# A written-out order of matrix work for all eight head pairs of a decoder layer

## The chip, the core and the metric

The kernel runs on one core of a Trainium2 chip. A core has a matrix engine (TensorE, PE in the profile; its weight loads are PEld), VectorE (DVE), ScalarE (ACT), GpSimd (POOL) and SyncE (SP), which here only issues DMAs. Each engine works through its own instructions in the order in which they stand, and waits on semaphores for the others. The metric is the device time of one execution in microseconds (us); the kernel before took 1234.75 us, the median of three runs (1234.38 to 1235.01).

## The reference, cut to what matters

One decoder layer over 1024 tokens of width 1024: a norm, one projection to the queries, keys and values of two groups of heads, both groups causal in blocks of 128 queries, an output projection, then a mixture of experts and a gated embedding.

```python
log_keep = jnp.where(strict, jax.nn.log_sigmoid(-z), 0.0)             # group 1: stick-breaking, 8 heads of 64
log_survive = lax.cumsum(log_keep, axis=3, reverse=True) - log_keep
weights = jnp.where(strict, jnp.exp(log_beta + log_survive), 0.0)
...
z = z - slopes[None, :, None, None, None] * dist                      # group 2: differential, 4 heads
probs = jax.nn.softmax(jnp.where(s_pos <= t_pos, z, -jnp.inf), axis=-1)
attn = probs[:, :, 0] - lam * probs[:, :, 1]
...
x = x + jnp.concatenate([_rmsnorm(o_sb), _rmsnorm(o_df)], axis=-1) @ w_out
```

`lam` comes from four vectors of 64 numbers. The results of each group are normed over their features before `w_out`, so sums of squares of the attention results are needed.

## The kernel before

**Pairs and units.** The attention is cut into eight pairs of 128 features. Pairs 0 to 3 hold two stick-breaking heads each, pairs 4 to 7 one differential head each (two score maps). A pair is cut into units of two query blocks (pr = 0 to 3, and by head in pairs 0 to 3). A unit has five kinds of TensorE work:

- score chunks (L361, L362, `z<-K,Qh`): each fills one of three PSUM banks. In pairs 0 to 3 ScalarE reads it twice (L404, L405), VectorE then scans the row (L408) and GpSimd multiplies (L409). In pairs 4 to 7 VectorE adds the distances and takes the maximum (L432), ScalarE takes the exponential (L439), and VectorE joins the two maps (L450).
- turns (L378, `tp<-ident,row`): the finished rows are transposed; ScalarE writes the upper part of the result (`wth`, L54), VectorE the rest (`wtl`, L55).
- values (L488 to L491, `pv<-wth,V` and `pv<-wtl,V`), which need both parts; ScalarE and VectorE evict their sum.
- the finish (L795, `z<-ones,sq`): a sum of squares of the result, after its store to `oT_d` in DRAM.
- beside these, the projections (L228 to L230, `mm<-hT,whi`): the values of this pair and the keys and queries of the next one. One item is six matmuls; four items fill a bank. Each weight matrix is split by ScalarE and VectorE (`wlo`, L201).

**The order.** For pairs 0 to 6 the class `Mix` writes out TensorE's order. It keeps an estimate of the time at which TensorE, ScalarE, VectorE and GpSimd come free, with fixed durations, and takes the next ready item from five queues; a projection is taken when its pair has a smaller share of projections done than of attention, or when nothing else is ready. `allowed` in `run_pairs` holds a unit's scores back until the second last unit is turned; for the first unit of pair 4 until the last unit of pair 3 is turned and pair 3 is finished. Every split and eviction stands behind all that the estimate has given its engine before. The order of the other engines is set by a scheduler with priorities; splits and evictions are raised by `k.boost`.

**Pair 7** is not in this list: when pairs 0 to 6 are done, `attend_items` and `run_items` emit its work beside the output projection's weights (`out_weights`, `woh` and `wol`) and leave TensorE's order to the scheduler. `out.normed(b)` reads `oT_d` back for 128 tokens, takes twelve small VectorE steps from the sums of squares to their inverse roots (L66 to L100), spreads these with transposes (L1130, L1136; L1134 and L1140 after the change), scales the rows (L1132, L1137) and splits them; the output projection (L1158 to L1160) follows.

**Shared places.** `k.sums` (sums of squares of pairs 0 to 3) and `k.dist` (the distances, a GpSimd iota and two VectorE instructions, L807 and L808) have one buffer in turn: `distances` runs when pair 4 begins and has to wait until pair 3's sums are read. `lambdas` runs there too, in a buffer of the ring of rows.

Of the kernel before, what the change touches and what calls it, by code (L numbers as in the profile page):

```python
# [133 lines left out]
def lambdas(k):  # L134
    nc, pool = k.nc, k.cp
    row = k.rows.tile([128, S], FT, name="row")
    lq = row[0:1, 0:256].rearrange("p (a n) -> p a n", a=4)
    for i, a in enumerate((k.lambda_q1, k.lambda_k1, k.lambda_q2, k.lambda_k2)):
        nc.sync.dma_start(lq[:, i, :], a)
    lp = row[0:1, 256:384].rearrange("p (a n) -> p a n", a=2)  # L140
    ls = row[0:1, 384:386]
    for i in range(2):
        nc.vector.tensor_tensor(lp[:, i, :], lq[:, 2 * i, :], lq[:, 2 * i + 1, :], OP.mult)
    nc.vector.reduce_sum(ls, lp, axis=AX)
    nc.scalar.activation(ls, ls, AF.Exp)
# [389 lines left out]
class Mix:  # L535
# [11 lines left out]
    def on(self, eng, ready, dur):  # L547
        self.at[eng] = max(self.at[eng], ready) + dur
        return self.at[eng]

# [25 lines left out]
    def do_s(self):  # L576
        u, c, f, n, last, x = self.S.pop(0)
        f()
        self.pe += c + 0.03
# [4 lines left out]
        if u.P.df:  # L584
            a = self.on("dve", self.pe, dve(w))
            if last:
                d = self.on("dve", a, 0.3)
                e = self.on("act", d, act(n))
                d = self.on("dve", e, 0.2)
# [34 lines left out]
    def do_v(self):  # L624
        u, g = self.V.pop(0)
        u.value(g)
        u.vals += 1
        self.nV += 1
        c = 0.7 if u.P.df else 0.47
        self.pe += c  # L630
        self.done["m", u.p] += c
        if g == u.pr:
            a = self.on("act", self.pe, 0.4)
            self.pvfree = [a if u.P.df else self.on("dve", a, 0.45)]
            u.out = self.pvfree[0]
# [5 lines left out]
    def do_f(self):  # L641
        u = self.F.pop(0)
        u.finish()
        self.on("act", self.pe, 0.4)
# [8 lines left out]
    def do_p(self):  # L653
# [6 lines left out]
        if kind == "last":  # L660
            a = self.on("act", self.pe, 1.2)
            self.mmfree = self.mmfree[1:] + [self.on("dve", a, 1.3)]

# [3 lines left out]

    def run(self):
# [3 lines left out]
        while left():  # L672
            ready = {x: get[x]() for x in left()}
# [13 lines left out]

def run_pairs(k, Ps, qk, n):

    mix = Mix(k, 3)  # L690
    us = [units_of(k, P) for P in Ps[:n]]
    every = [u for x in us for u in x]
# [9 lines left out]

    for p in range(n):
        P, Q = Ps[p], Ps[p + 1]
        v0, v1 = value_projection(k, P)
# [28 lines left out]
        for x in range(2):  # L734
            kd, c, f, ok = turns[x]
            turns[x] = (kd, c, lambda f=f, p=p, x=x: (f(), state["v"].__setitem__((p, x), True)), ok)
        K = group_items(k, lambda Q=Q: Q.W[0], HALVES, evac_k(k, Q))
        QQ = group_items(k, lambda Q=Q: Q.W[1], HALVES, evac_q(k, Q, Q.qscale))
# [10 lines left out]
    for x, u in enumerate(every):  # L749
        near = 1 if u.p == 4 and (u.pr, u.h) == (0, 0) else 2  # L750
        before = every[x - near] if x >= near else None

        def allowed(u=u, before=before, near=near):
            if state["kq"] < u.p or not (before is None or before.turns == before.pr + 1):
                return False
            return near == 2 or not (mix.F and mix.F[0].p < u.p)

        u.allowed = allowed
    return mix
# [18 lines left out]
def finish_o(k, ot, P, pr):  # L778
    nc = k.nc
    q = slice(pr * 256, (pr + 1) * 256)  # L780
    nc.sync.dma_start(k.oT_d[P.ch][:, q], ot)
    if P.df or P.ch:
        sq = k.wk.tile([128, 256], FT, name="sq", bufs=2)
    else:
        sq = k.sums[:, q]
    nc.scalar.activation(sq, ot, AF.Square)
    if not P.df:
        if P.ch:
            nc.gpsimd.tensor_tensor(k.sums[:, q], k.sums[:, q], sq, OP.add)
        if P.ch < 3:  # L790
            return
        sq = k.sums[:, q]
    ps = bank_z(k, P.df)
# [152 lines left out]
def phase_attention(k, moe, pq):  # L946
# [34 lines left out]
    k.nz = 0  # L981
    k.sums = c1.tile([128, S], FT, name="sums")
    k.ss = c1.tile([128, NB, 5], FT, name="ss")
# [3 lines left out]
    def first(p):  # L987
        if p == 1:
            anchor.extend((k.last_hi, k.last_lo) + ((k.last_raw,) if hasattr(k, "last_raw") else ()))
        if p == 4:  # L990
            distances(k)
            lambdas(k)

    mix = run_pairs(k, Ps, qk, 7)
    for u in (mix.S[0][0], *(x[0] for x in mix.S)):
# [16 lines left out]
    v0, v1 = value_projection(k, P)  # L1012
    wo = out_weights(k)
    with ExitStack() as es:
        for x in anchor:
            es.enter_context(tc.issue_after(x.ins))
        out.constants()
    run_items(items[:ends["v"]], v0, wo[:4])
    out.space(0)
    run_items(items[ends["v"]:ends[0]], v1, wo[4:])  # L1020
    out.space(1)
    mid = ends[0] + 2
    run_items(items[ends[0]:mid])
# [976 lines left out]
```

## Time and profile before

| | us |
|---|---|
| median of 3 runs | 1234.75 |
| the profiled execution's own time | 1239.4 |
| its span on the core | 1237.6 |
| TensorE busy in the span | 1154.6 (93%) |
| VectorE busy | 923.6 (75%) |
| ScalarE busy | 721.7 (58%) |
| GpSimd busy | 207.6 (17%) |

The attention of pairs 0 to 3 takes the span from about 40 to 328 us, that of pairs 4 to 7 from 328 to about 597; the output projection runs from 543, the experts from about 715, and the last part from about 1130. A matmul counts as busy until its modelled end, so a busy TensorE can still be slow: the granted clock (PEclk, 1.00 is 2.4 GHz, 0.50 is 1.2 GHz) has to be read beside it.

### The profile page before, as it was taken

How to read it: one execution, taken by the hardware profiler on the slowest of the kernel's cores; microseconds unless marked ns; L12 is line 12 of the kernel's file. 1: busy time of each engine (PE TensorE's matmuls, PEld its weight loads, DVE VectorE, ACT ScalarE, POOL GpSimd, SP SyncE). 2: the span in 40 equal slices, each digit the busy share in tenths (PEclk: the TensorE clock that was granted, in tenths of full speed). 3: DMA queues.
4: the chain of work that ended last, by engine and by line, in shares of the span. 5: the costliest groups of instructions: out<-in, count | busy, mean ns of one | idle time of the engine just before them, and what ended most of it. 6: DMA issues, size and time to landing. Idle time of an engine off the chain costs nothing. (4 is left out here: it accounts for less than half of the span.)

```text
span 1237.6 us, 22827 instructions
## 1 busy us (share of the span) xinstructions
PE 1154.6 (93%) x8181; PEld 831.4 (67%) x8181; DVE 923.6 (75%) x2144; ACT 721.7 (58%) x1408; POOL 207.6 (17%) x298
## 2 busy tenths in 40 slices
PE   5999999999898999989789899999999999997996
PEld 4766666666556666655445488898998989883443
DVE  7577787868466676878797776787878878865875
ACT  6476767666456666743332355676767767653432
POOL 0033433434100000001321111121111211110000
PEclk9999999999998999989899989999999999998999
DMA  6212121211120122523674879899999999947721
GB/s 206 66 30 73 30 73 31 63 36 48 51 75 25 47 61 58 170 71 110 222 216 139 285 229 290 264 341 291 284 324 289 325 292 316 313 135 290 246 77 51
DMA packets 211756, 202.54 MB, mean 164 GB/s; under 512 B 12697, under 2 KB 182681, under 8 KB 211642
## 3 DMA queue, kind: packets, MB, share of 16 engines
q1 hardware_dynamic: 205688, 180.22, 47.1%
q0 software_dynamic: 5808, 20.58, 4.4%
q8 instruction: 65, 1.06, 0.3%
q14 instruction: 49, 0.40, 0.1%
q10 hardware_dynamic: 146, 0.27, 0.1%
HBM read 163.03 MB, written 29.62 MB: 156 GB/s over the span
## 5 line engine op out<-in xcount | busy, mean ns | idle before, releaser
L228 PE MATMUL mm<-hT,whi 128*128 128x512 f32 (+1 forms) x416 | 216.7, 522 | 2.5 <-DVE rs_v L66 1.4
L229 PE MATMUL mm<-hT,whi 128*128 128x512 bf16 (+1 forms) x416 | 157.8, 379 | 4.3 <-DVE hT L184 4.3
L230 PE MATMUL mm<-hT,wlo 128*128 128x512 bf16 (+1 forms) x416 | 156.6, 377 | 0.0
L1607 PE MATMUL gu<-xh,mhiu 128*128 128x128 f32 (+4 forms) x512 | 155.7, 315 | 0.0
L1607 PE MATMUL gu<-xh,mhig 128*128 128x128 f32 (+4 forms) x512 | 154.6, 309 | 0.1
L1609 PE MATMUL gu<-xbl,mhig 128*128 128x128 bf16 (+4 forms) x512 | 125.2, 244 | 2.6 <-DVE xbl L1520 2.6
L1609 PE MATMUL gu<-xbl,mhiu 128*128 128x128 bf16 (+4 forms) x512 | 124.7, 244 | 0.0
L1610 PE MATMUL gu<-xh,mblg 128*128 128x128 bf16 (+4 forms) x512 | 120.1, 235 | 0.0
L1610 PE MATMUL gu<-xh,mblu 128*128 128x128 bf16 (+4 forms) x512 | 119.5, 233 | 0.0
L55 DVE TENSOR_TENSOR mdl<-mrawd,mdh 128x1024 bf16<-128x1024 f32 x63 | 77.0, 1221 | 44.6 <-ACT mdh L54 44.6
L228 PEld LDWEIGHTS mm<-hT,whi 128*128 128x128 f32 x416 | 80.8, 194 | 33.9 <-ACT hT L183 1.9
L54 ACT ACTIVATE wth<-tp 128x512 fp32r<-128x512 f32 (+2 forms) x168 | 71.0, 449 | 55.8 <-PE tp L378 36.2
L55 DVE TENSOR_TENSOR wtl<-tp,wth 128x512 fp32r<-128x512 f32 (+2 forms) x168 | 79.2, 492 | 32.2 <-ACT wth L54 30.9
L409 POOL TENSOR_TENSOR row<-row,keep 128x127 f32<-128x127 f32 (+3 forms) x64 | 77.0, 1204 | 147.0 <-DVE keep L408 90.8
L229 PEld LDWEIGHTS <-whi 128*128 128x128 bf16 x416 | 40.8, 98 | 88.2 <-issue 83.4
L1607 PEld LDWEIGHTS gu<-xh,mhig 128*128 128x128 f32 x512 | 98.1, 192 | 0.9 <-ACT xh L1519 0.5
L55 DVE TENSOR_TENSOR mblg<-mrawg,mhig 128x1024 bf16<-128x1024 f32 x62 | 75.8, 1223 | 30.3 <-ACT mhig L54 29.2
L54 ACT ACTIVATE mdh<-mrawd 128x1024 fp32r<-128x1024 f32 x64 | 67.5, 1055 | 51.7 <-PE ya L1639 47.1
L408 DVE TENSOR_TENSOR_SCAN keep<-keep,zx 128x128 f32<-128x128 f32 (+3 forms) x64 | 85.7, 1346 | 15.5 <-ACT keep L404 15.0
L1607 PEld LDWEIGHTS gu<-xh,mhiu 128*128 128x128 f32 x512 | 97.1, 190 | 0.0
L46 POOL DMA_INDIRECT y_d<-yo,put x27 | 44.5, 1649 | 290.0 <-ACT yo L1657 185.8
L54 ACT ACTIVATE mhig<-mrawg 128x1024 fp32r<-128x1024 f32 x64 | 67.4, 1053 | 20.5 <-PE gu L1610 11.8
(348 smaller groups left out, 3358.7 us busy)
## 6 DMA issues: line engine op xcount, KB each, us to landing
mrawg<-in_w_expert_gate_dram SPq DMA_DIRECT2D x64, 512.0 KB, 5.9
mrawu<-in_w_expert_up_dram SPq DMA_DIRECT2D x64, 512.0 KB, 6.7
mrawd<-in_w_expert_down_dram SPq DMA_DIRECT2D x64, 512.0 KB, 3.7
wraw<-in_w_in_dram SPq DMA_DIRECT2D x24, 512.0 KB, 4.1
yg<-y_d SPq DMA_DIRECT2D x16, 512.0 KB, 5.9
xt<-in_x_dram SPq DMA_DIRECT2D x8, 512.0 KB
oT_d<-ot SPq DMA_DIRECT2D x32, 128.0 KB, 2.9
wraw<-in_w_out_dram SPq DMA_DIRECT2D x8, 512.0 KB, 3.8
```

The lines of the kernel that those rows point to most:

```text
L46: i = k.nc.gpsimd.indirect_dma_start(out=out, out_offset=bass.IndirectOffsetOnAxis(ap=idx, axis=0), in_=src, in_offset=None)
L54: nc.scalar.activation(hi, src, AF.Copy)
L55: (eng or nc.vector).tensor_tensor(lo, src, hi.bitcast(FT), OP.subtract)
L228: nc.tensor.matmul(ps, hi[:, c, :], hT[:, c % 4, :], start=(c == 0), stop=False)
L229: nc.tensor.matmul(ps, wv[:, c, :], k.hT[half][2][:, c, o:o + n], start=False, stop=False)
L230: nc.tensor.matmul(ps, lo[:, c, :], hv[:, c % 4, :], start=False, stop=(c == NC - 1))
L408: nc.vector.tensor_tensor_scan(a, a, k.zeros.to_broadcast([128, n]), 1.0, op0=OP.mult, op1=OP.add)
L409: nc.gpsimd.tensor_tensor(beta[:, :n - 1], beta[:, :n - 1], keep[:, 1:n], OP.mult)
L1607: nc.tensor.matmul(ps[:, x], hi[:, c], xh[:, c], start=(c == 0), stop=False)
L1609: nc.tensor.matmul(ps[:, x], hv[:, c], xl[:, c], start=False, stop=False)
L1610: nc.tensor.matmul(ps[:, x], bl[:, c], xv[:, c], start=False, stop=(c == NC - 1))
```

## The change

Three edits. The sums of squares go to two buffers of their own and the lambdas to a third (these are later taken by the first output weights), and the distances keep a buffer of their own and are made before the first pair. The special rule for pair 4 goes. `Mix` gets a new rule in `on`: a split or eviction marked `first` ends at most 0.7 us later than it would on a free engine, while it still adds its duration to its engine; three small durations of VectorE in the estimate get shorter. And pair 7 joins `Mix`, with its value projection and the output weights in the queue of projections; its items after the finish of its first unit are recorded (`emit`) and emitted beside the output projection.

```diff
 def lambdas(k):
-    row = k.rows.tile([128, S], FT, name="row")
+    row = k.base.tile([128, 512], FT, name="lam", tag="wol2")
...
+    def on(self, eng, ready, dur, first=False):
+        start = max(self.at[eng], ready)
+        self.at[eng] = start + dur
+        return (min(start, ready + 0.7) if first else start) + dur
...
-        u.turn(g)
+        self.emit(0.44, lambda: u.turn(g))
...
-        a = self.on("act", self.pe, 0.6)
-        d = self.on("dve", a, 0.75)
+        a = self.on("act", self.pe, 0.6, True)
+        d = self.on("dve", a, 0.7, True)
...
-            self.pvfree = [a if u.P.df else self.on("dve", a, 0.45)]
+            self.pvfree = [a if u.P.df else self.on("dve", a, 0.45, True)]
...
-    us = [units_of(k, P) for P in Ps[:n]]
+    us = [units_of(k, P) for P in Ps[:n + 1]]
...
+        if p == n:
+            items = group(v0[:4], None, nothing) + [turns[0]] + [("mid", 0.0, f, None) for f in last[0]]
+            items += group(v1[:4], None, nothing) + [turns[1]] + [("mid", 0.0, f, None) for f in last[1]]
...
-        near = 1 if u.p == 4 and (u.pr, u.h) == (0, 0) else 2
-        before = every[x - near] if x >= near else None
...
+        before = every[x - 2] if x >= 2 else None
+        u.allowed = lambda u=u, before=before: state["kq"] >= u.p and (before is None or before.turns == before.pr + 1)
...
-    k.dist = k.ac.tile([128, S], FT, name="sums")
+    k.dist = k.ac.tile([128, S], FT, name="dist")
...
-    k.sums = c1.tile([128, S], FT, name="sums")
+    k.sums = [k.base.tile([128, 512], FT, name=f"sums{x}", tag=f"wol{x}") for x in range(2)]
...
+    distances(k)
+    mix = run_pairs(k, Ps, qk, 7, last)
...
-        mix.run()
-    P = Ps[7]
-    items, ends = attend_items(k, P)
...
+        mix.run(lambda: not mix.P and len(mix.F) <= 3)
+    rest = []
+    mix.emit = lambda c, f: rest.append((c, f))
+    mix.run(lambda: len(mix.F) <= 2)
+    mid = len(rest)
+    mix.run()
     out.normed(0)
-    run_items(items[mid:ends[1]], out.items(0)[1:])
-    run_items(items[ends[1]:], out.items(1) + out.items(2))
+    run_items(rest[:mid], out.items(0)[1:])
+    run_items(rest[mid:], out.items(1) + out.items(2))
```

Place A is on TensorE, in pair 1, at the second head's unit of query blocks 4 and 5: its first turns (`tp`) and its first values (`pv`); the `mm` rows between are projections, ten rows to an item. Before:

```order
L378 MATMUL tp<-ident,row 128x128 x8
L361 MATMUL z<-K_789,Qh_791 128x512
L362 MATMUL z<-K_789,Ql_793 128x512
L364 LDWEIGHTS identb
L364 MATMUL z<-maskb,identb 128x128
L361 MATMUL z<-K_789,Qh_791 128x512
L362 MATMUL z<-K_789,Ql_793 128x512
...
L488 MATMUL pv<-wth,V_796 128x256
L489 MATMUL pv<-wtl,V_796 128x256
```

After the change:

```order
L361 MATMUL z<-K_804,Qh_806 128x512
L362 MATMUL z<-K_804,Ql_808 128x512
L364 LDWEIGHTS identb
L364 MATMUL z<-maskb,identb 128x128
L378 MATMUL tp<-ident,row 128x128 x8
L361 MATMUL z<-K_804,Qh_806 128x512
L362 MATMUL z<-K_804,Ql_808 128x512
...
L488 MATMUL pv<-wth,V_811 128x256
L489 MATMUL pv<-wtl,V_811 128x256
```

Between turns and values stood two score chunks and four projection items (forty rows), and now one chunk and two items (twenty rows).

Place B is on TensorE where pair 3 ends and pair 4 begins; the 256-column chunks without a mask are pair 4's first, L795 is pair 3's last finish. Before:

```order
L795 MATMUL z<-ones,sums 128x1 x2
L361 MATMUL z<-K_3063,Qh_3065 128x256
L362 MATMUL z<-K_3063,Ql_3067 128x256
L361 MATMUL z<-K_3064,Qh_3066 128x256
L362 MATMUL z<-K_3064,Ql_3068 128x256
L361 MATMUL zx<-K_3063,Qh_3065 128x256
L362 MATMUL zx<-K_3063,Ql_3067 128x256
```

After the change:

```order
L488 MATMUL pv<-wth,V_2358 128x256
L489 MATMUL pv<-wtl,V_2358 128x256
L361 MATMUL z<-K_3110,Qh_3112 128x256
L362 MATMUL z<-K_3110,Ql_3114 128x256
L361 MATMUL z<-K_3111,Qh_3113 128x256
L362 MATMUL z<-K_3111,Ql_3115 128x256
L361 MATMUL zx<-K_3110,Qh_3112 128x256
L362 MATMUL zx<-K_3110,Ql_3114 128x256
L488 MATMUL pv<-wth,V_2358 128x256
L489 MATMUL pv<-wtl,V_2358 128x256
```

Pair 4's first scores stood behind all of pair 3, and now stand between values of pair 3's last units but one, with that pair's last unit (its turns and values) still to come.

Place C is on TensorE, from a finish of pair 7 to the first transposes of the output stage (`rs_y`). Before:

```order
L795 MATMUL z<-ones,sq 128x1 x2
L361 MATMUL zx<-K_5159,Qh_5161 128x384
L362 MATMUL zx<-K_5159,Ql_5163 128x384
L361 MATMUL z<-K_5159,Qh_5161 128x512
L362 MATMUL z<-K_5159,Ql_5163 128x512
...
L361 MATMUL z<-K_5159,Qh_5161 128x512
L362 MATMUL z<-K_5159,Ql_5163 128x512
L1130 MATMUL tp<-ident,rs_y 128x128
```

After the change:

```order
L800 MATMUL zx<-ones,sq 128x1 x2
L361 MATMUL z<-K_5148,Qh_5150 128x384
L362 MATMUL z<-K_5148,Ql_5152 128x384
...
L361 MATMUL zx<-K_5148,Qh_5150 128x384
L362 MATMUL zx<-K_5148,Ql_5152 128x384
L1134 MATMUL tp<-ident,rs_y 128x128
L1140 MATMUL tp<-ident,rs_y 128x128 x4
L378 MATMUL tp<-ident,row 128x128 x4
```

Before, this was the finish of pair 7's second unit, and all its scores were done at the first transpose. Now it is the finish of its first unit, with four score chunks between, and the second unit's turns and values and seven score chunks follow behind the transpose.

## Rows read from the trace of the kernel before

**Rows 1.** The page's second part: granted clock, in 40 slices of the span.

```profile
PEclk9999999999998999989899989999999999998999
```

**Rows 2.** Stretches: length; PE, PEld, DVE, ACT, POOL busy (instructions); granted clock; DMA share; GB/s.

```profile
40.00:320.00 280.00, 271.30 (x1615) 179.70 (x1614) 204.92 (x294) 185.60 (x438) 97.19 (x137) 1.00 0.20 52
320.00:360.00 40.00, 35.33 (x171) 20.77 (x170) 23.60 (x76) 21.05 (x49) 2.99 (x9) 0.91 0.16 43
380.00:400.00 20.00, 15.21 (x88) 13.49 (x87) 15.45 (x59) 13.75 (x33) 0.80 (x4) 0.83 0.11 34
500.00:544.00 44.00, 36.95 (x175) 26.18 (x173) 36.64 (x137) 29.90 (x65) 1.41 (x8) 0.84 0.43 139
544.00:600.00 56.00, 53.31 (x296) 32.11 (x294) 43.66 (x167) 20.80 (x42) 6.62 (x11) 0.97 0.38 123
600.00:720.00 120.00, 101.61 (x541) 56.79 (x540) 97.94 (x384) 39.06 (x80) 27.69 (x28) 0.93 0.66 219
```

**Rows 3.** TensorE's waits from 40 to 320 us: total, times, longest.

```profile
PE z L361 <- ACT row L405: 3.4, 3, 1.2
PE pv L489 <- DVE wtl L55: 2.3, 5, 0.8
```

**Rows 4.** TensorE in order of time at pair 4's first scores; idle and releaser in brackets.

```profile
332.51 0.58 PE L361 MATMUL z<-K,Qh 128*128 128x256 f32 x1 [2.70 <-DVE dfm L432]
...
341.70 0.44 PE L378 MATMUL tp<-ident,row 128*128 128x128 f32 x2 [1.62 <-DVE dfm L438]
```

**Rows 5.** VectorE in order of time at the same place: the distances, the first reduction.

```profile
329.98 0.69 DVE L807 TENSOR_SCALAR row<-sums 128x1024 f32<-128x1024 f32 x1 [1.43 <-POOL sums L804]
...
332.15 0.29 DVE L432 CUSTOM_DVE_ANT_0 row<-z,sums 128x128 f32<-128x128 f32 x1 [0.15 <-DVE sums L808]
```

**Rows 6.** TensorE in order of time where pair 4's last unit is turned.

```profile
387.49 0.30 PE L378 MATMUL tp<-ident,row 128*128 128x128 f32 x1 [0.93 <-DVE dfm L437]
391.49 0.90 PE L378 MATMUL tp<-ident,row 128*128 128x128 f32 x3 [3.71 <-DVE row L450]
```

**Rows 7.** TensorE in order of time at place A in pair 1.

```profile
159.28 1.04 PE L378 MATMUL tp<-ident,row 128*128 128x128 f32 x8
...
160.66 0.48 PE L361 MATMUL z<-K,Qh 128*128 128x512 f32 x1
...
161.21 0.39 PE L228 MATMUL mm<-hT,whi 128*128 128x512 f32 x1
...
166.55 0.48 PE L488 MATMUL pv<-wth,V 128*128 128x256 f32 x1
```

**Rows 8.** VectorE in order of time at the same place.

```profile
162.14 1.93 DVE L201 TENSOR_TENSOR wlo<-wraw,whi 128x1024 bf16<-128x1024 f32 x1
...
164.83 1.29 DVE L55 TENSOR_TENSOR wtl<-tp,wth 128x512 fp32r<-128x512 f32 x2
```

**Rows 9.** The weight split L201: count, shortest/median/longest ns, first and last start.

```profile
L201 DVE TENSOR_TENSOR wlo<-wraw,whi x24: 1208/1226/2159, 11.8 to 475.1; 128x1024 bf16<-128x1024 f32 x24
```

**Rows 10.** TensorE in order of time from pair 7's first finish to the output projection.

```profile
523.75 1.01 PE L795 MATMUL z<-ones,sq 128*128 128x1 f32 x4 [0.62 <-ACT sq L786]
...
539.92 0.32 PE L1130 MATMUL tp<-ident,rs_y 128*128 128x128 f32 x1 [0.79 <-DVE rs_y L100]
...
543.44 0.50 PE L1158 MATMUL mm<-woh,od 128*128 128x512 f32 x1 [0.44 <-ACT od L54]
```

**Rows 11.** VectorE in order of time ahead of that transpose.

```profile
529.97 1.22 DVE L1058 TENSOR_TENSOR wol<-wraw,woh 128x1024 bf16<-128x1024 f32 x1
...
531.43 0.55 DVE L432 CUSTOM_DVE_ANT_0 keep<-z,sums 128x384 f32<-128x384 f32 x1
...
531.97 0.17 DVE L66 TENSOR_SCALAR rs_v<-ss 128x10 f32<-128x10 f32 x1
...
539.70 0.17 DVE L100 SCALAR_TENSOR_TENSOR rs_y<-rs_i,rs_y 128x10 f32<-128x10 f32 x1
```

**Rows 12.** ScalarE in order of time in the first stage: first key eviction.

```profile
24.01 0.36 ACT L251 ACTIVATE K<-mm 64x256 fp32r<-64x256 f32 x1
```

More of the change, by code (lines that the diff above doesn't have):

```diff
@@ L545, in __init__ @@
         self.nT = self.nV = 0
-    def on(self, eng, ready, dur):
-        self.at[eng] = max(self.at[eng], ready) + dur
-        return self.at[eng]
+        self.emit = lambda c, f: f()
+    def on(self, eng, ready, dur, first=False):
+        start = max(self.at[eng], ready)
+        self.at[eng] = start + dur
+        return (min(start, ready + 0.7) if first else start) + dur
     def add_pair(self, P, p, units, proj):
@@ L577, in do_s @@
         u, c, f, n, last, x = self.S.pop(0)
-        f()
+        self.emit(c, f)
         self.pe += c + 0.03
@@ L586, in do_s @@
             if last:
-                d = self.on("dve", a, 0.3)
+                d = self.on("dve", a, 0.2)
                 e = self.on("act", d, act(n))
-                d = self.on("dve", e, 0.2)
+                d = self.on("dve", e, 0.15)
                 if x < len(chunks_of(n)):
@@ L625, in do_v @@
         u, g = self.V.pop(0)
-        u.value(g)
+        c = 0.7 if u.P.df else 0.47
+        self.emit(c, lambda: u.value(g))
         u.vals += 1
         self.nV += 1
-        c = 0.7 if u.P.df else 0.47
         self.pe += c
@@ L632, in do_v @@
         if g == u.pr:
-            a = self.on("act", self.pe, 0.4)
-            self.pvfree = [a if u.P.df else self.on("dve", a, 0.45)]
+            a = self.on("act", self.pe, 0.4, True)
+            self.pvfree = [a if u.P.df else self.on("dve", a, 0.45, True)]
             u.out = self.pvfree[0]
@@ L642, in do_f @@
         u = self.F.pop(0)
-        u.finish()
+        self.emit(0.11, u.finish)
         self.on("act", self.pe, 0.4)
@@ L660, in do_p @@
         if kind == "last":
-            a = self.on("act", self.pe, 1.2)
-            self.mmfree = self.mmfree[1:] + [self.on("dve", a, 1.3)]
+            a = self.on("act", self.pe, 1.2, True)
+            self.mmfree = self.mmfree[1:] + [self.on("dve", a, 1.3, True)]
     def share(self, what, p):
@@ L666, in share, with run @@
         return p + (self.done[what, p] / t if t else 1.0)
-    def run(self):
+    def run(self, until=lambda: False):
         do = {"v": self.do_v, "t": self.do_t, "s": self.do_s, "f": self.do_f, "p": self.do_p}
@@ L671, in run @@
         left = lambda: {x: q for x, q in zip("vtsfp", (self.V, self.T, self.S, self.F, self.P)) if q}
-        while left():
+        while left() and not until():
             ready = {x: get[x]() for x in left()}
@@ L685, in run, with run_pairs @@
             do[pick]()
-def run_pairs(k, Ps, qk, n):
+def run_pairs(k, Ps, qk, n, last):
     mix = Mix(k, 3)
-    us = [units_of(k, P) for P in Ps[:n]]
+    us = [units_of(k, P) for P in Ps[:n + 1]]
     every = [u for x in us for u in x]
@@ L701, in proj @@
         return out
-    for p in range(n):
-        P, Q = Ps[p], Ps[p + 1]
+    for p in range(n + 1):
+        P, Q = Ps[p], Ps[min(p + 1, n)]
         v0, v1 = value_projection(k, P)
@@ L736, in run_pairs @@
             turns[x] = (kd, c, lambda f=f, p=p, x=x: (f(), state["v"].__setitem__((p, x), True)), ok)
+        for u in us[p]:
+            u.values = lambda g, p=p: (p, g // 2) in state["v"]
+        if p == n:
+            items = group(v0[:4], None, nothing) + [turns[0]] + [("mid", 0.0, f, None) for f in last[0]]
+            items += group(v1[:4], None, nothing) + [turns[1]] + [("mid", 0.0, f, None) for f in last[1]]
+            mix.add_pair(P, p, us[p], items)
+            break
         K = group_items(k, lambda Q=Q: Q.W[0], HALVES, evac_k(k, Q))
@@ L749, in run_pairs @@
     for x, u in enumerate(every):
-        near = 1 if u.p == 4 and (u.pr, u.h) == (0, 0) else 2
-        before = every[x - near] if x >= near else None
[L753 to L758, printed above, removed]
+        before = every[x - 2] if x >= 2 else None
+        u.allowed = lambda u=u, before=before: state["kq"] >= u.p and (before is None or before.turns == before.pr + 1)
     return mix
@@ L781, in finish_o @@
     nc.sync.dma_start(k.oT_d[P.ch][:, q], ot)
+    sums = k.sums[pr // 2][:, pr % 2 * 256:pr % 2 * 256 + 256]
     if P.df or P.ch:
@@ L784, in finish_o @@
     else:
-        sq = k.sums[:, q]
+        sq = sums
     nc.scalar.activation(sq, ot, AF.Square)
@@ L788, in finish_o @@
         if P.ch:
-            nc.gpsimd.tensor_tensor(k.sums[:, q], k.sums[:, q], sq, OP.add)
+            nc.gpsimd.tensor_tensor(sums, sums, sq, OP.add)
         if P.ch < 3:
             return
-        sq = k.sums[:, q]
+        sq = sums
     ps = bank_z(k, P.df)
@@ L990, in first, with out_constants @@
         if p == 4:
-            distances(k)
             lambdas(k)
-    mix = run_pairs(k, Ps, qk, 7)
+    def out_constants():
+        with ExitStack() as es:
+            for x in anchor:
+                es.enter_context(tc.issue_after(x.ins))
+            out.constants()
+    wo = [f for _, f in out_weights(k)]
+    last = [[out_constants] + wo[:4] + [lambda: out.space(0)], wo[4:] + [lambda: out.space(1)]]
+    distances(k)
+    mix = run_pairs(k, Ps, qk, 7, last)
     for u in (mix.S[0][0], *(x[0] for x in mix.S)):
@@ L1008, in phase_attention @@
     with tc.manual_schedule(engines={mybir.EngineType.PE}):
-        mix.run()
-    P = Ps[7]
-    items, ends = attend_items(k, P)
[L1012 to L1023, printed above, removed]
+        mix.run(lambda: not mix.P and len(mix.F) <= 3)
[4 more added lines that the diff above has]
+    mix.run()
     out.normed(0)
-    run_items(items[mid:ends[1]], out.items(0)[1:])
-    run_items(items[ends[1]:], out.items(1) + out.items(2))
+    run_items(rest[:mid], out.items(0)[1:])
+    run_items(rest[mid:], out.items(1) + out.items(2))
     k.right.close()
```

## The prediction

> **What bounds the kernel now.** I read the page's totals first: TensorE is busy for 1154.6 of 1237.6 us of span, VectorE for 923.6. Then the slices of the granted clock [rows 1]: nearly all nines, with an eight where TensorE had stood still. So the kernel is bound by TensorE, and what can be won is its idle time and the half speed that follows. Third, the stretches [rows 2]: from 40 to 320 us (pairs 0 to 3) TensorE is busy for 271.30 of 280 us at clock 1.00, which leaves 8.7 us over eight units of each pair. The places with a loss are three: 320 to 360 (pair 3 to 4), 380 to 400 (pair 4 to 5), and 500 to 544 (pair 7 and the start of the output stage). Last, I read the engines in order of time at these places.
>
> The profiled execution took 1239.4 us, 4.65 more than the median of 1234.75. The sum is made against its stretches and is then taken off the median.
>
> **Pair 3 to 4: -7.0 us.** Pair 4's first scores wait 2.70 us for a reduction [rows 4], the reduction waits for the distances, and these wait for the iota, which GpSimd could only write when the old sums had been read [rows 5]. A second wait, 1.62 us, follows [rows 4]. In the 40 us, 40 - 35.33 = 4.67 are idle, and 0.09 of the clock is 3.6: 8.3 lost [rows 2]. With a place of its own the distances are there long before, and the order puts pair 4's scores between pair 3's last values (place B), where two other units still have work. Late next is the ordinary chain of a softmax, which has something beside it now; I leave 1.3 for it. Bounds: 8.3 gained, or nothing if values of pair 3 wait there instead.
>
> **Pair 4 to 5: -7.0.** TensorE waits 0.93 and 3.71 us for the last rows of pair 4 [rows 6]; its projections are used up by then, and only turns and values are left. 4.8 idle and 0.17 of 20 us, 3.4, are lost: 8.2 [rows 2]. In the new order two groups of projection items stand between the unit's last scores and its last turns: four items took 166.55 - 161.21 = 5.34 us in pair 1 [rows 7], more than the longest wait. I leave 1.2. Bounds: 8.2, or nothing.
>
> **Pair 7 and the output stage: -3.0.** In 44 us, 7.05 idle and 0.16 of the clock, 7.0: 14.1 lost [rows 2]. Ahead of place C the written order should recover most. But at place C only four score chunks are left between the finish of pair 7's first unit and the first normed transpose, against all of the second unit's rest before, when 16.2 us lay between [rows 10]. From the finish's result VectorE took 7.90 us over the twelve small steps (531.97 to 539.87), with other work between them [rows 11]. Of that work now four reductions of 0.55 (2.2) and one split of 1.22 stand there, with twelve steps of 0.17 (2.0): 5.4 at the least, 7.9 as before; I take 6.6, about the middle, since joined rows come in between too. Four chunks give TensorE 4 x 0.55 (160.66 to 161.21, one chunk) [rows 7] = 2.2: a wait of about 4.5 us in place of 0.79 [rows 10]. The second transposes wait for the scaled rows, as the output projection did for 0.44 [rows 10]; VectorE now has the second unit's rows and lower parts queued there (1.29 a pair [rows 8], twice: 2.6). With 1.2 of small waits and 2.7 of clock, 11 us of loss remain. Bounds: -7 if the moved turns and scores slide in as soon as they are ready, +3 if both waits cost the clock too. The moved items themselves only change places on TensorE.
>
> **Values nearer to their turns: +6.0.** The new estimate lets a lower part end 0.7 us after it is ready at the latest, though VectorE works in its own order. At place A, in pairs 1 to 3: before, the turns start at 159.28 and the values at 166.55, and nothing waits, though VectorE starts the weight split (1.93 us) at 162.14 and the two lower parts at 164.83 only, the first ready at about 164.83 + 1.29/2 = 165.5 [rows 7, 8]. After, one chunk (0.55) comes ahead of the turns, and two items (2.7) are between: the turns start at 159.83, the values at 159.83 + 1.38 + 2.67 = 163.9. Wait: 1.6 us, three times, 4.8. It is 0 if VectorE takes the lower part ahead of the split, and 2.2 if both lower parts are needed. One such place in pair 0 I price a little lower (1.3), and the unit after, whose values move less, at about half (0.75, three times: 2.2), 8.3 in all. Values waited for 2.3 us in all before, 0.8 at most, and scores 3.4 us on the ScalarE row [rows 3]; of the latter 2.3 go, since there is one less chunk in a block. That leaves 6.0; bounds 0 (below it, -3, if those waits go and no new ones come) and 11.
>
> The split's own price sets this stall: it takes 1208 to 2159 ns, 1226 in the middle [rows 9], and at place A 1.93 [rows 8]; GpSimd is busy for 97.19 of the 280 us there [rows 2]. The Trainium skill, "GPSIMD Engine Reference", section "1. Specifications", says that GpSimd's SBUF interfaces are shared with VectorE and that instructions with two SBUF inputs contend for them; the split is one, and the trace agrees. Without that contention the place would cost 0.7 less a time, 2 us in all.
>
> **The rest: +1.9.** The lambdas' loads and their exponential move to the first stage, on ScalarE's queue between the squares; something like the 0.36 of a small eviction [rows 12] with its wait, +0.4 (0 to 1.5). Distances and sums cost the same instructions elsewhere. Behind 544 us VectorE gets the work of the moved items: seven reductions from 0.55 up (4.5), two pairs of lower parts at 1.29 (2.6), two joined rows (about 1.7), 8.8 us [rows 8, 11]. It is busy there for 43.66 of 56 us, and for 97.94 of 120 in the stretch after [rows 2]: 12.3 us are free in the first. I take +1.5, the work that I expect late; bounds 0 and 8.8.
>
> **Sum:** -7.0 - 7.0 - 3.0 + 6.0 + 0.4 + 1.5 = -9.1, hence 1234.75 - 9.1 = 1225.6 us; by itself 1216 to 1238.
>
> **The rivals.** *Slower: the value waits cost the clock as well.* The two waits of 2.70 and 1.62 us [rows 4] stand in a stretch whose clock lost 3.6 us [rows 2], 1.8 each: TensorE's granted level fell from 2.4 to 1.2 GHz after them. Today pairs 0 to 3 hold 1.00, with no wait over 1.2 us [rows 2, 3]. If place A and its like give more than five waits above that, this decides: six times 1.8 = 10.8, 4 us of stalls that I had netted out, and no gain at place C (3): 1225.6 + 17.8 = 1243.4. For it speaks the 1.6 us worked out above, against it that VectorE is busy for only 204.92 of 280 us there and may come earlier. The Trainium skill, "TensorE: Matmul & The Clock Gate", section "A second HAM failure mode: psum-queue depth-cycling", tells of the same loss: frequent short idles between groups of matmuls that make the clock swing. The trace agrees as far as its two waits go; by the page the slower case would be the likely one, at about 1243.
>
> *No change: VectorE behind 544 us.* If all 8.8 us come on the path instead of 1.5, and half of the gain at place C goes, it is 1225.6 + 7.3 + 1.5 = 1234.4. Against it are the free 12.3 us; for it, that the output projection waits on these very engines from its first matmul.
>
> *It does not do what it says at pair 4 to 5*: the items are used up earlier in fact than in the list, since TensorE runs ahead elsewhere, and the gap stays: 1225.6 + 7.0 = 1232.6.
>
> *A larger gain:* the values find their lower parts ready (0.5 instead of 6.0), place C is filled by the moved items (-7), tail 0.9, pairs 3 to 5 as above but 4 and 5 whole: -7.0 - 8.2 - 7.0 + 0.5 + 0.4 + 0.9 = -20.4, 1214.4.
>
> **How the numbers follow.** Forecast 0.46, larger gain 0.18, no change 0.11, the gap that stays 0.05, slower 0.20. About 0.2%, 2.5 us, is what can be told from no change here: 1232.3 to 1237.2. Of the forecast 0.44 lie below that and 0.02 in it; of no change 0.02 below, 0.07 in, 0.02 above; of the gap that stays 0.02 and 0.03; the other two lie outside. Faster 0.66, same 0.12, slower 0.22. The range of 8 in 10 is 1211 to 1243: it leaves out the far end of the larger gain (some 0.07) and the upper half of the slower case (0.1).
>
> **What would show it.** Around pair 3 to 4 no wait over 1.3 us and a clock near 1.00; between pair 4's last scores and last turns projections, and no wait of 3 us. At place A a wait of the values on the lower part (`wtl`, L55) of 1 to 2 us in each of pairs 1 to 3: with a clock of 1.00 from 40 to 320 us the forecast holds, with 0.95 the slower case does. Ahead of the first normed transpose (L1134) a wait of 3 to 6 us. The forecast is wrong if the stretch from 40 to 320 us loses over 10 us, or if the output stage ends more than 5 us later against its start.

## The result, and the profile after

The changed kernel took 1229.23 us (median of 7 runs, 1227.77 to 1231.84) where the kernel before, beside it, took 1235.47 (7 runs, 1234.38 to 1236.67): 0.995 of it, 95% interval 0.9937 to 0.9964, or 6.2 us less. A second set on another occasion gave 0.9937 (0.9924 to 0.9949). The forecast was 9.1 us less, 1225.6, in a range of 1211 to 1243.

The two profiled executions stand further apart, 1239.4 and 1227.81 us. From pair 0's first scores to the last matmul of the output projection it is 53.6 to 687.1 us before and 51.8 to 677.5 after: 633.5 against 625.7, so 7.8 of the 11.6 us lie in what was changed. The other 3.8 lie ahead of it (1.8) and behind it (2.0). Behind it both kernels do the same work; ahead of it only the lambdas and the distances were moved in, so this part says little about the change.

The slices of the granted clock after the change, to be held against [rows 1]:

```profile
PEclk9999999999999999879899999999999999999999
```

A slice is about 31 us long. The eight at 371 to 402 us (pair 4 to 5) is gone; the loss at pair 3 to 4 showed as no eight before, since it lay across two slices. An eight and a seven now stand from 490 to 552 us, around the start of the output stage; the seven is lower than anything before. The same stretches as in [rows 2], with the same columns (length; PE, PEld, DVE, ACT, POOL busy; granted clock; DMA share; GB/s):

```profile
40.00:320.00 280.00, 266.15 (x1570) 176.34 (x1568) 205.11 (x296) 185.47 (x434) 96.37 (x138) 0.99 0.19 49
280.00:320.00 40.00, 37.03 (x211) 24.53 (x209) 28.90 (x39) 24.67 (x54) 14.23 (x15) 0.96 0.15 39
320.00:360.00 40.00, 39.57 (x214) 24.79 (x214) 27.42 (x93) 26.19 (x61) 2.20 (x9) 1.00 0.20 58
380.00:400.00 20.00, 20.00 (x125) 14.43 (x123) 12.24 (x46) 12.31 (x32) 1.06 (x6) 1.00 0.13 40
500.00:544.00 44.00, 34.73 (x161) 24.02 (x159) 31.02 (x99) 22.19 (x47) 1.27 (x7) 0.77 0.31 102
544.00:600.00 56.00, 51.85 (x303) 33.13 (x301) 50.72 (x198) 26.82 (x52) 15.28 (x15) 1.00 0.53 177
```

The two stretches at pairs 3 to 5 have lost nearly all of their loss: 8.3 us fell to 0.4, and 8.2 to nothing. From 40 to 320 us the idle time grew from 8.7 to 13.9 us, and the clock fell once (0.96 over 40 us, 1.6 us). From 500 to 544 us it is 9.3 idle and 0.23 x 44 = 10.1 of clock: 19.4, where it was 14.1 before. The two windows do not hold the same work, since the changed kernel is some 10 us ahead there: its first matmul of the output projection comes at 530.9, not 543.4 us. From 400 us to that matmul TensorE loses 15.4 us before (8.5 idle, 6.8 of clock) and 21.5 after (12.7 and 8.7), so the loss stands by this count as well. Three of the priced terms came as forecast, and that of pair 7 went the other way. The waits of TensorE from 40 to 320 us (total, times, longest) show what [rows 3] turned into:

```profile
PE pv L489 <- DVE wtl L55: 7.6, 8, 1.4
PE tp L378 <- DVE wtl L55: 2.8, 1, 2.8
```

The scores' waits for ScalarE's rows are gone, and values wait for lower parts eight times; a turn of pair 3 (at 297.80 us) waits 2.8 us for one. At place A in pair 1, TensorE after (start, length, idle and releaser in brackets; compare [rows 7]):

```profile
157.26 1.04 PE L378 MATMUL tp<-ident,row 128*128 128x128 f32 x8
...
161.17 0.48 PE L488 MATMUL pv<-wth,V 128*128 128x256 f32 x1
163.00 0.38 PE L489 MATMUL pv<-wtl,V 128*128 128x256 f32 x1 [1.36 <-DVE wtl L55]
```

and VectorE there (compare [rows 8]):

```profile
159.57 1.93 DVE L201 TENSOR_TENSOR wlo<-wraw,whi 128x1024 bf16<-128x1024 f32 x1
161.53 0.69 DVE L252 TENSOR_TENSOR K<-mm,K 64x512 fp32r<-64x512 f32 x1
162.26 1.29 DVE L55 TENSOR_TENSOR wtl<-tp,wth 128x512 fp32r<-128x512 f32 x2
```

The values stand 3.9 us behind the turns, where it was 7.3, and VectorE still takes the weight split of 1.93 us first: a wait of 1.36. The new loss at 500 to 544 us is this, on TensorE (line numbers are five higher after the change, L800 is the finish):

```profile
508.38 0.60 PE L283 MATMUL mm<-ident,vt 128*128 128x128 f32 x4
513.84 1.01 PE L800 MATMUL zx<-ones,sq 128*128 128x1 f32 x4 [4.87 <-ACT sq L791]
...
522.85 0.69 PE L361 MATMUL zx<-K,Qh 128*128 128x384 f32 x1 [1.69 <-DVE dfm L432]
...
526.50 0.48 PE L1134 MATMUL tp<-ident,rs_y 128*128 128x128 f32 x1 [0.98 <-DVE rs_y L100]
```

The wait of 4.87 us is that of the finish of pair 6's last unit, ahead of place C; it waits for a square. On ScalarE that square's input was there at 508.0:

```profile
507.65 0.38 ACT L499 ACTIVATE ot<-pv 128x256 f32<-128x256 f32 x1
...
511.49 2.00 ACT L1061 ACTIVATE woh<-wraw 128x1024 fp32r<-128x1024 f32 x2
513.38 0.41 ACT L791 ACTIVATE sq<-ot 128x256 f32<-128x256 f32 x1
...
519.94 0.15 ACT L801 ACTIVATE ss<-zx 128x2 f32<-128x2 f32 x1
```

Between the input and the square stand exponentials, evictions, and two splits of the output weights. (The last row is the sum of squares of pair 7's first unit; it is used below.) What followed ran at 1.2 GHz:

```profile
513.50:534.00 20.50, 15.75 (x52) 11.45 (x52) 15.81 (x57) 9.42 (x19) 0.00 (x0) 0.50 0.28 83
```

Until this wait the clock had been 1.00 since 302 us; it fell after the 4.87 us and stayed low through the smaller waits of the list. VectorE ended the twelve small steps ahead of L1134 here:

```profile
526.28 0.17 DVE L100 SCALAR_TENSOR_TENSOR rs_y<-rs_i,rs_y 128x10 f32<-128x10 f32 x1
```

### The profile page after: what moved, and what is told of

It is laid out like the page before. It is cut to its first block, busy times and chain, and to the rows that moved or that the text cites. A ratio compares the mean times of both kernels' runs of the same rounds, so it can differ in the third digit from the quotient of the medians.

```text
span 1226.0 us, 22814 instructions
## 1 busy us (share of the span) xinstructions
PE 1145.5 (93%) x8181; PEld 826.5 (67%) x8181; DVE 923.1 (75%) x2144; ACT 723.0 (59%) x1408; POOL 207.5 (17%) x298
## 3 DMA queue, kind: packets, MB, share of 16 engines
q8 instruction: 65, 1.06, 0.3%
## 5 line engine op out<-in xcount | busy, mean ns | idle before, releaser
L228 PE MATMUL mm<-hT,whi 128*128 128x512 f32 (+1 forms) x416 | 210.9, 508 | 2.6 <-DVE rs_v L66 1.4
L409 POOL TENSOR_TENSOR row<-row,keep 128x127 f32<-128x127 f32 (+3 forms) x64 | 77.9, 1218 | 143.5 <-DVE keep L408 88.4
L228 PEld LDWEIGHTS mm<-hT,whi 128*128 128x128 f32 x416 | 80.2, 193 | 30.9 <-ACT hT L183 2.0
L54 ACT ACTIVATE mdh<-mrawd 128x1024 fp32r<-128x1024 f32 x64 | 67.6, 1056 | 51.8 <-PE ya L1643 47.6
L408 DVE TENSOR_TENSOR_SCAN keep<-keep,zx 128x128 f32<-128x128 f32 (+3 forms) x64 | 85.4, 1346 | 14.1 <-ACT keep L404 13.4
```

The costliest lines, as they stand in the source:

```text
L54: nc.scalar.activation(hi, src, AF.Copy)
L228: nc.tensor.matmul(ps, hi[:, c, :], hT[:, c % 4, :], start=(c == 0), stop=False)
L408: nc.vector.tensor_tensor_scan(a, a, k.zeros.to_broadcast([128, n]), 1.0, op0=OP.mult, op1=OP.add)
L409: nc.gpsimd.tensor_tensor(beta[:, :n - 1], beta[:, :n - 1], keep[:, 1:n], OP.mult)
```

## The experiments

Each run stands beside runs of the kernel before on the same chip; ratios are to these, and the intervals hold 95%. The theory was that each edit acts where the prediction put it; its numbers were the terms of the sum. The value of an edit is the difference of two ratios times 1237 us (about the time of the kernel before in these sets).

| run | ratio to before | interval |
|---|---|---|
| the changed kernel | 0.9950 | 0.9937 to 0.9964 |
| the changed kernel again | 0.9937 | 0.9924 to 0.9949 |
| first edit alone | 0.9903 | 0.9884 to 0.9922 |
| first edit, rule for pair 4 kept | 0.9941 | 0.9926 to 0.9956 |
| first edit and square first | 0.9879 | 0.9862 to 0.9897 |
| changed, `first` off | 0.9966 | 0.9950 to 0.9982 |
| changed, `first` for pairs 4 to 7 | 0.9934 | 0.9914 to 0.9953 |
| changed, old estimate in pairs 0 to 3 | 0.9876 | 0.9861 to 0.9890 |
| changed, square first | 0.9904 | 0.9884 to 0.9924 |
| changed, output weights late | 0.9901 | 0.9881 to 0.9920 |
| both repairs | 0.9856 | 0.9838 to 0.9875 |
| both repairs, weights late | 0.9858 | 0.9835 to 0.9880 |
| both repairs, weights spread | 0.9976 | 0.9966 to 0.9986 |

### The first edit alone

The kernel before with the three places and without the rule for pair 4:

```diff
-    k.sums = c1.tile([128, S], FT, name="sums")
+    k.sums = [k.base.tile([128, 512], FT, name=f"sums{x}", tag=f"wol{x}") for x in range(2)]
...
-        near = 1 if u.p == 4 and (u.pr, u.h) == (0, 0) else 2
+        before = every[x - 2] if x >= 2 else None
```

> The kernel before with the first edit alone: sums, distances and lambdas in places of their own, distances made before the first pair, no special rule for pair 4; the estimate and pair 7 stay as they were. Theory (each edit acts where the prediction put it): the 2.70 and 1.62 us waits at pair 4's first scores go and the clock stays 1.00 from 320 to 360 us, the 3.71 us wait for pair 4's last rows stays; 7 us less than before, about 1228.5. Rival (the new estimate is what brings pair 4's scores forward, the places alone only shift the wait to pair 3's last values): within 2.5 us of before, 1233 to 1236, and an idle time over 2 us shows between 315 and 340 us.

Measured: 1224.63 us (6 runs), 0.9903, 12 us less than before. That is more than the theory's 7 and more than the whole change. The rival falls. In its trace the turns of pair 4's last unit waited 3.71 us before [rows 6]; now nothing there waits longer than 1.31 us:

```profile
371.60 0.66 PE L283 MATMUL mm<-ident,vt 128*128 128x128 f32 x4 [1.31 <-ACT vt L278]
...
381.52 0.66 PE L378 MATMUL tp<-ident,row 128*128 128x128 f32 x4 [1.11 <-DVE wtl L55]
```

So the second term of the sum, too, belongs to this edit, and the other two together cost 4 to 6 us. The places have a price of their own: a finish of pair 3 now waits 2.2 us for a score chunk of pair 4 to leave its bank (311.66 us in this trace).

### The places without the order

The same with the rule kept, so that TensorE's order up to the experts is that of before.

```diff
+        near = 1 if u.p == 4 and (u.pr, u.h) == (0, 0) else 2
```

> The kernel before with sums, distances and lambdas in places of their own and distances made before the first pair, but with the special rule for pair 4 kept, so that TensorE's order is exactly that of before. Theory (two causes: the distances' wait is 4 us with its clock, and the rule, which holds pair 4's first scores back while projections go on, uses up the projections that are missing at pair 4 to 5): the 2.70 us wait at pair 4's first scores shrinks under 1 us, the 3.71 us wait at pair 4's last turns stays, 0.995 to 0.997 of before. Rival (the late distances alone shifted all of pair 4): both waits go, as with the first edit whole, 0.990 to 0.992.

Measured: 1230.42 us (6 runs), 0.9941. TensorE at pair 4, from its first turns to its last:

```profile
335.49 0.44 PE L378 MATMUL tp<-ident,row 128*128 128x128 f32 x2 [0.80 <-DVE row L450]
...
379.75 0.30 PE L378 MATMUL tp<-ident,row 128*128 128x128 f32 x1 [0.94 <-DVE dfm L437]
383.76 1.76 PE L378 MATMUL tp<-ident,row 128*128 128x128 f32 x7 [3.71 <-DVE row L450]
```

The theory holds at the place: the wait of 2.70 us is gone and the 3.71 us is there, to the hundredth. The distances' wait was worth 7 us (0.59%), more than the 4 to 6 of the theory, though the interval reaches into that range. Taking the rule away as well is worth 4.7 us (0.9941 to 0.9903), and it removes the gap at pair 4 to 5: from 370 to 390 us TensorE takes 12 matmuls of L228 (projections) without the rule and 3 with it. The rule had held pair 4's scores back while projections went on.

### The new estimate

```diff
-        return (min(start, ready + 0.7) if first else start) + dur
+        return start + dur
```

> The changed kernel with the mark `first` without effect: places and pair 7 as after, every split and eviction behind all that its engine was given, as before. Theory: the value waits of pairs 0 to 3 go (5 to 7 us back), the 3.71 us wait with its clock at pair 4 to 5 returns (7 to 8 us lost), pair 7 stays as after: 1228 to 1231, the same as after within 2.5. Rival (the new estimate carries the gain): 1234 to 1237.

Measured: 1231.9 us (12 runs), 0.9966, between the two expectations, 2 to 4 us above the changed kernel's two ratios. The gap at pair 4 to 5 did not come back, for the reason just shown. With `first` for pairs 4 to 7 alone:

```diff
-        a = self.on("act", self.pe, 0.6, True)
-        d = self.on("dve", a, 0.7, True)
+        a = self.on("act", self.pe, 0.6, u.P.df)
+        d = self.on("dve", a, 0.7, u.P.df)
...
```

(The same edit stands at the evictions of values and projections.)

> The changed kernel with `first` for pairs 4 to 7 alone; pairs 0 to 3 count their splits and evictions as before. Theory: the waits of values on wtl in pairs 0 to 3 (7.6 us in 8 waits after the change), the 2.8 us wait of a turn at 297.8 and the half-speed stretch behind it go, pairs 4 to 7 stay: 5 to 7 us less than after, 1222 to 1224. Rival (TensorE only waits elsewhere in those pairs, for the ScalarE rows as before, 3.4 us, and pair 4 starts later): within 2.5 us of after, 1227 to 1231.

Measured: 1228.74 us (6 runs), 0.9934: the rival's size. The waits on lower parts had gone from 7.6 us only to 5.5, in ten:

```profile
PE pv L489 <- DVE wtl L55: 5.5, 10, 1.0
PE mm L283 <- ACT vt L278: 1.8, 3, 0.7
```

TensorE's order in pairs 0 to 2 still was not that of before, since the change also writes 0.7 us for a lower part where 0.75 stood. Setting that back as well, for pairs 0 to 3 (the diff is against the run just shown):

```diff
-        d = self.on("dve", a, 0.7, u.P.df)
+        d = self.on("dve", a, 0.7 if u.P.df else 0.75, u.P.df)
```

> The changed kernel with the old estimate for pairs 0 to 3 in full (no `first`, 0.75 us for a lower part); there TensorE's order is again that of the kernel before, and pairs 4 to 7 keep the new one. Theory (the new estimate costs pairs 0 to 3 what the trace shows as waits on wtl, and the 0.05 us shorter lower part in it is enough for half of that, which is why `first` off alone gave back 2 us): idle time from pair 0's first scores to pair 4's first falls from 13.3 to about 7.5 us with no half-speed stretch, 6 to 7 us less than after: 0.989 to 0.990 of before. Rival (the estimate's early values pay later, since more projections are left for pairs 4 and 5): 0.993 to 0.995.

Measured: 1222.05 us (4 runs), 0.9876, while the changed kernel in the same set had 0.9937: 7.5 us less. The theory holds in its cause, with a gain at the upper end of what it gave or above; but it expected no half-speed stretch, and from 280 to 320 us the clock is 0.96 here too, behind the 2.2 us of the last row. The waits from 40 to 320 us are those of [rows 3] again, with one for a finish of pair 3, as in the first edit's trace:

```profile
PE z L361 <- ACT row L405: 3.4, 3, 1.2
PE pv L489 <- DVE wtl L55: 2.3, 5, 0.9
PE z L800 <- DVE dfm L432: 2.2, 1, 2.2
```

The changed kernel's second run:

> The changed kernel once more, beside the runs below on one chip, and for a second profile of it. Both theories: 0.995 of before, give or take 0.002; the 4.9 us wait for the square at pair 6's last finish and the eight waits of values on wtl in pairs 0 to 3 are there again.

Measured: 1228.96 us (5 runs), 0.9937. It has the wait for the square (4.87 us) and the eight waits of values (7.6 us in all) again. Its clock from 280 to 320 us is 1.00 in spite of a turn's wait of 2.85 us there, so the half-speed stretch that the first profile shows behind that wait is not in every execution.

### The square and the output weights

```diff
-    nc.scalar.activation(sq, ot, AF.Square)
+    with k.tc.high_priority(offset=k.boost):
+        nc.scalar.activation(sq, ot, AF.Square)
```

> The changed kernel with one thing more: the square ahead of a finish (ScalarE, sq<-ot) gets the priority of splits and evictions. TensorE's order is unchanged up to the output stage. Theory: the 4.87 us wait at pair 6's last finish (513.84) is ScalarE's queue, where the square ran 5.4 us after its input was evicted, behind exponentials and two woh splits; the wait shrinks to under 2 us and the half-speed stretch behind it (20.5 us) to half: 6 us less than after, about 1223. Rival (the next score chunks and values wait for the same VectorE rows, so the wait moves by a few instructions): within 2.5 us of after, 1227 to 1231.

Measured: 1224.78 us (6 runs), 0.9904: 4 to 6 us less than the changed kernel by its two sets. (The edit raises the square of every finish, not of this one alone.) The finish does not wait at all, and the waits behind it are 0.93, 1.44 and 1.79 us, far less than the 4.87; TensorE, and the stretch:

```profile
508.35 0.50 PE L801 MATMUL zx<-ones,sq 128*128 128x1 f32 x4
511.43 0.44 PE L361 MATMUL z<-K,Qh 128*128 128x384 f32 x1 [0.93 <-DVE dfm L432]
513.91 0.61 PE L801 MATMUL zx<-ones,sq 128*128 128x1 f32 x4 [1.44 <-ACT ss L802]
...
521.36 0.48 PE L1135 MATMUL tp<-ident,rs_y 128*128 128x128 f32 x1 [1.79 <-DVE rs_y L100]
```

```profile
500.00:544.00 44.00, 37.21 (x182) 24.21 (x181) 31.94 (x110) 22.47 (x50) 1.26 (x7) 0.84 0.37 125
```

The theory holds for the wait, and the loss of the stretch falls from 19.4 to 6.8 + 7.0 = 13.8 us; but the clock's share falls by 3 us of 10, not by half. The splits' part in the queue, by their priority alone:

```diff
-        nc.scalar.activation(k.woh[c], raw, AF.Copy)
...
+        with k.tc.high_priority(offset=-k.boost if c > 3 else 0):
+            nc.scalar.activation(k.woh[c], raw, AF.Copy)
...
```

> The changed kernel with the last four splits of the output weights behind other work of their time on ScalarE and VectorE (lower priority), nothing else; the square keeps its own. Theory (the splits, emitted four at once and not counted in the estimate, make the queue): the square is past two splits of 1.0 us each, the 4.9 us wait at pair 6's last finish shrinks by 2 to 3 us, and 2 to 4 us go in all: 0.992 of before. Rival (the exponentials ahead of the square make the queue, the splits are only in its company): the wait stays over 4 us, 0.994 to 0.996.

Measured: 1226.08 us (6 runs), 0.9901, 4.5 us less than the changed kernel beside it. TensorE at the finish and behind it:

```profile
512.90 0.61 PE L800 MATMUL zx<-ones,sq 128*128 128x1 f32 x4 [2.97 <-ACT sq L791]
...
524.06 0.69 PE L361 MATMUL zx<-K,Qh 128*128 128x384 f32 x1 [3.95 <-DVE dfm L432]
```

Two splits of 1.0 us out of the way take 1.9 off the wait, so they made two fifths of it, and the exponentials and evictions that still stand there made the rest; but a score chunk waits 3.95 us now, where 1.69 was the longest such wait, and VectorE took two splits of the output weights around that time (519.25 and 522.17 us). In the first edit's kernel, where the scheduler places pair 7, the same priority was expected to take away the finishes' waits:

> The kernel before with the first edit (own places) and the square's higher priority. Theory (the square waits behind the splits in any version, but pair 7 outside of the written order spreads these, so less is to be had): the finishes' waits of 0.62 and 1.34 us at the start of the output stage go, 2 to 4 us less than the first edit alone: 0.987 to 0.988 of before. Rival (the normed transposes end that stage, whatever the finishes do): as the first edit alone, 0.990, within 0.0015.

Measured: 1223.63 us (5 runs), 0.9879. The ratio moved by 3 us, but the waits of 0.62 and 1.33 us for the square are still in the trace. At the second, its input is evicted right before it; at the first, a split of 1.05 us still stands between (509.86 us). The theory is not shown, and the intervals overlap.

### Both repairs

The old estimate for pairs 0 to 3, and the square first.

> The changed kernel with the old estimate for pairs 0 to 3 and the higher priority of the square together. Theory (the two losses are independent: 7 us less in pairs 0 to 3, 4 to 5 us at pair 6's last finish): 0.983 to 0.985 of before, the fastest so far, about 1217 to 1219. Rival (what is won ahead of the output stage is lost to its DMAs and VectorE behind it): 0.987, as the old estimate alone.

Measured: 1218.93 us (4 runs), 0.9856 (0.9838 to 0.9875). It is the fastest so far, 18 us ahead of the kernel before and 10 to 12 ahead of the changed one. The sum of the single gains (7.5 and 4 to 6 off 0.9937) would be 0.983 to 0.985; it falls a little short of that, within the interval. Its losses from 320 to 360 and 380 to 400 us are 0.1 us and none. With the weights at lower priority as well:

> Both repairs, and the last four splits of the output weights at lower priority on ScalarE and VectorE, as in the run of that edit alone. Theory (the splits are part of the queue that the inverse roots and score chunks still wait in, 1.79, 1.44 and 0.93 us with the square alone): 1 to 3 us less than both repairs, 0.982 to 0.985 of before. Rival (with the square gone ahead the splits hide elsewhere, and put late they only hold the output projection): 0.985 to 0.988.

Measured: 1218.06 us (5 runs), 0.9858: the rival, nothing more to be had by that. And with the splits one by one in the list:

```diff
+            def apart():
+                return mix.pe >= at[0] + 3.5
...
+            def spread(f):
+                return ("mid", 0.0, lambda: (f(), at.__setitem__(0, mix.pe)), apart)
+            w = [spread(f) for f in last[0][1:5] + last[1][:4]]
...
```

> As both repairs, and the splits of the output weights stand in the list one by one, at least 3.5 us of the estimate apart, instead of four and four; the written order then ends later, and holds pair 7's second unit whole. Theory (what is left at the start of the output stage, 6.8 us idle and 5.2 us of clock with the square alone, is VectorE's queue of four splits and the normed transposes that stand too early): 3 to 5 us less than both repairs, 0.980 to 0.982. Rival (the inverse roots now wait behind the second unit, and the output projection starts later for it): as both repairs or up to 3 us slower.

Measured: 1234.17 us (12 runs), 0.9976, 15 us slower than both repairs: neither theory. The written list ended one unit later, and the first matmul of the output projection came at 540.06 us, against 519 with both repairs. On the way there TensorE waited for the rows of single units:

```profile
521.78 0.50 PE L361 MATMUL z<-K,Qh 128*128 128x512 f32 x1 [0.85 <-DVE dfm L432]
525.37 1.76 PE L378 MATMUL tp<-ident,row 128*128 128x128 f32 x7 [2.20 <-DVE row L450]
...
540.06 0.80 PE L1174 MATMUL mm<-woh,od 128*128 128x512 f32 x1
```

The run spreads the splits and ends the list later at once, so it does not tell the two apart. It suggests that the early normed transposes of place C, which the prediction had priced as a loss, keep that stage going; that is not shown by itself.

## Why the prediction was right, and where it was not

**Pair 3 to 4** (-7.0): right. The window lost 8.3 and now 0.4; the places alone, with the order unchanged, gave 7 us.

**Pair 4 to 5** (-7.0): by the window the size was right, 8.2 recovered; by the runs, taking the rule away was worth 4.7 us. The missing projections were the cause, as the prediction had it, and it was the special rule that had used them up, not anything of the estimate.

**Values nearer to their turns** (+6.0): the size was right, 5.2 us of idle time and 1.6 of clock in the first profile, 7.5 by the runs; 1.36 at place A where 1.6 was worked out. The unit after, put at half of a wait of 1.5 (0.75), waits 1.06 in pairs 1 and 2, behind a second split that takes 2.84 us there (why, is told in the last section). In pair 3 the wait fell on a turn, 2.8 us. The cause was only in part the one named: `first` off in those pairs gave back 2 us at most, and the rest came when the 0.05 us that the estimate takes off a lower part was put back too, a number that the prediction passed over (with `first` on it was not run). The rival that these waits cost the clock as well fell: from 40 to 280 us it stayed at 1.00 with waits up to 1.4 us. By the reading of the page of the Trainium skill that the prediction held against it ("TensorE: Matmul & The Clock Gate", "A second HAM failure mode: psum-queue depth-cycling") it would have swung; no such swing shows at these waits, and the measurement decides.

**Pair 7 and the output stage** (-3.0): this step failed. "Ahead of place C the written order should recover most" did not happen; the stretch lost 5.3 us more (6.1 from 400 us to the output projection). The wait came one step earlier than the one priced, at pair 6's last finish: the list puts the finish 1.0 us after its result by an estimate that charges nothing for eight output-weight splits, and the scheduler puts its square behind two of them. At L1134 itself it was 0.98 us, not 4.5. VectorE's time there was priced well: from the finish's result (520.1) to the end of the twelve steps (526.4) it took 6.4 us, where the sum had 6.6; but TensorE spent it in three waits, 1.69, 0.66 and 0.98, and in chunks at half the clock. (The 7.9 us of before that the 6.6 leans on began at 532.0, 7 us behind that finish's own result at 525.0, so it was not the time from the result.) The mis-sized term is worth 8 to 9 us in its stretch.

**The rest** (+1.9): too dear. Between the first and the last matmul of the output projection (543.4 to 687.1 us before, 530.9 to 677.5 after) TensorE loses 16.6 us idle and 6.8 to the clock before, and 13.9 and 6.6 after: 3 less, where 1.5 more was put down; the runs do not show which of the moved items filled that idle time. That made up for part of what the failed step cost: 6.2 to 7.8 us less instead of 9.1. So it is in part luck that the total came this near: the last two terms missed by 8 to 9 and by some 4 us, with opposite signs.

**Its own signs.** Those at pairs 3 to 5 came. Those at place A came in pairs 1 and 2, with a clock of 0.99 from 40 to 320 us. The wait of 3 to 6 us ahead of L1134 did not come. "Loses over 10 us" from 40 to 320 us can only mean over 10 us more than before, since the sum itself allowed 8.7 + 6.0; it lost 15.5 in all, 6.8 more.

## What to carry to other kernels

A written order is as good as the queue that it doesn't model: whatever it prices at nothing (here a square without priority and eight weight splits) is where the next wait stands, and the page shows it as one long wait behind a tiny instruction. Undo each part of such a change by itself: here the smallest edit alone gave 12 us and all three together 6 to 8, and with the cap `first` off in pairs 0 to 3 a constant changed by 0.05 us was worth 7 us (0.9934 against 0.9876). A gap is often made far ahead of where it shows: the 3.71 us at pair 4 to 5 came from projections that a rule, by holding scores back, had spent up to some 60 us earlier.

## What the runs showed of the hardware

**The clock after a wait.** The granted clock did not answer to the length of a wait alone. It stayed at 1.00 behind waits of up to 1.4 us from 40 to 280 us. The turn's wait of 2.8 us stands in four traces: in two the clock stayed at 1.00 (the changed kernel's second run and with the square first), and in two it fell, at a loss of 1.7 us (the first run and with the output weights late). A finish's wait of 2.2 us stands in eight traces, and in five of them the clock fell, again at a loss of 1.7 us. So single profiles differ by such a fall where the kernel is the same. Behind 4.87 us, where more waits followed, it fell for 20.5 us.

**VectorE beside GpSimd.** The weight split L201 (VectorE) reads two tensors, and so does GpSimd's multiply L409. After the change the two met in either order:

```profile
112.00 1.20 DVE L201 TENSOR_TENSOR wlo<-wraw,whi 128x1024 bf16<-128x1024 f32 x1
112.25 2.80 POOL L409 TENSOR_TENSOR row<-row,keep 128x1023 f32<-128x1023 f32 x1 [2.30 <-PE z L364]
...
176.83 2.00 POOL L409 TENSOR_TENSOR row<-row,keep 128x1023 f32<-128x1023 f32 x1 [3.15 <-DVE keep L408]
177.06 2.84 DVE L201 TENSOR_TENSOR wlo<-wraw,whi 128x1024 bf16<-128x1024 f32 x1 [0.41 <-ACT whi L195]
```

The one that starts first keeps its own length (1.20 and 2.00 us), and the other gets longer. In the two traces, before and after, the 30 weight splits (L201) that no multiply overlaps take 1.21 to 1.23 us. The 17 that start during a multiply take 1.35 to 2.84, and each ends 1.07 to 1.09 us behind that multiply's end, whatever the overlap, as if it had stood still until the multiply was done. At place A that is 1.93 us before and after (multiply from 161.22 and from 158.65 us, 1.77 each), as the prediction held. The change moved the second split of pairs 1 and 2 to the start of a multiply: 2.84 where it took 2.15 before.
